# Weight sums, form sums and column statistics moved between engines in the first stage of a 1-core streaming-encoder block

## The chip, the cores and the metric

The kernel runs on one core of a Trainium2 chip (trn2). The metric is the device time of one execution in microseconds; the time before is the median of three runs. The core has five engines that run their own instruction queues in order: TensorE (PE in the profile; PEld are its weight loads), VectorE (DVE), ScalarE (ACT), GpSimd (POOL) and SyncE (SP), the last of which only issues transfers. GpSimd issues transfers too, among them those that add into their destination.

## The reference, cut to what matters

One encoder block on 1024 tokens of width 1024: RMS norm, one wide input projection, windowed attention with sinks on one branch, a chunked gated MLP on the other, two merge gates, an output projection, a residual and a last RMS norm. The change touches the head of the kernel only: the norm, the product for `vs`, its Gelu, and the mean and variance of each token over the 1024 columns of Gelu(vs), which the layer norm ahead of the spatial gating needs.

```python
h = rmsnorm(x, norm_g)
q, k, v, za, u, vs, zs, gm = split(h @ w_in)
v = layernorm(gelu(vs), ln_g, ln_b)          # mean and variance over 1024 columns per token
mixed = einsum('gij,bnjgc->bnigc', masked(w_s), v_blocks) + b_s
sgo = (gelu(u) * mixed * silu(zs)) @ w_sg_out
```

## The kernel before, in words

**Arithmetic.** Every fp32 operand is split into two parts: hi (a cast to fp32r on ScalarE, L177) and lo (the rest, a subtraction on VectorE, L178); a product is three matmuls (hi hi, hi lo, lo hi). Most products of the kernel use a scheme with seven block products in place of eight (Strassen's in Winograd's order); sums of blocks are formed first, by VectorE, by GpSimd, or by a transfer that adds into its destination (`add_to`, L226).

**The head.** The tokens are eight tiles of 128 (x0 to x7). Each is loaded (`load_x`, L575) into a `wr` tile (three buffers in rotation, shared with the weights), squared and summed on ScalarE (`scale_of`, L648), scaled on VectorE (L654), transposed on TensorE (L659), and evicted from PSUM by ScalarE and VectorE: hi and lo parts for the products (L665, L666) and fp32 copies f11, f12, f21, f22 for the block sums (L678; they lie in T_t3l, T_t4h, T_t4l, T_t3h). `vs_gemm` (L682 under it) multiplies tiles 0 to 4 with the first half of the columns. The weights of `vs` are eight tiles of 128x1024: W0 to W3 for the first 512 columns, W4 to W7 for the last.

**The forms.** Then an order written out by hand (`tc.manual_schedule` for TensorE, ScalarE and VectorE) makes the rest: `plain` multiplies tiles 0 and 4 with W4 to W7 (ps_sc), and for the pairs of tiles (1,5), (2,6), (3,7) `take` does five products called t1, t2, t3, b22 and t4, each in two halves c = 0, 1, 36 matmuls in all, with an evicting step behind the second half. Each form needs the split of a token sum (T_t1 = f11 - f12, T_t2 = -(f22 + T_t1), T_t3 = f22 - f12, T_b22, T_t4 = the difference `last` of what then stands in f11 and f21) and of two weight sums. The weight sums live in `chain`: two `s` tiles that start as W4 and W5 and are split and then added to by a transfer (`of_chain(c, nxt)`: split, then add W_nxt): W4, then +W6 (first form), +W0 (second form), +W2 (b22). An add has to wait until the split before it has read the tile. `ask` loads a raw weight or a sum of two into a `wr` tile, `of_raw` splits the next of these.

**Statistics.** `bn_stats` on VectorE (L858) makes the column statistics of a half row of xh (the tile of Gelu(vs)); `bn_aggr` (L1028) joins them. `normalize` (L1040 on VectorE, L1036 on ScalarE) needs all of them, and the mixing matmuls (`mix`, L1075) need the normalized xh. The next stage is the product for u (`gemm_pair`, L396), whose hooks run normalization, the bias of the mixing (`bias_of`) and the mixes.

**What sets the order.** Inside `manual_schedule` the three engines keep the program's order; GpSimd and SP, and all engines outside, are ordered by the scheduler. Transfers that make sums of later weights in DRAM (`early`, L339 on GpSimd's queue, shown as sums<-in_w_dram) are issued one at a time by `part_of_early` and held to a place among TensorE's matmuls (`paced`).

## Time and profile before

| what | value |
|---|---|
| time before | 917.69 us, median of 3 runs (916.05 to 919.14) |
| the profiled execution, its own time | 919.23 us |
| its span, first to last instruction | 917.2 us |
| busy: PE, DVE, ACT, POOL | 894.8, 710.7, 542.1, 162.3 us |
| instructions | 13264 |
| granted clock of TensorE, mean | 0.992 |
| chain that ended last | PE 91%, DMA 4%, DVE 2%, ACT 2%, issue 1% |

The chain is followed back from the last instruction to whatever released each step; TensorE makes up 91% of it, so the kernel is bound by TensorE, and other engines count where TensorE waits for them. In the rows of the profile, `wh` and `wl` are the hi and lo part of a weight, `T_t2h` and `T_t2l` those of the second form's token sum, and so on; `a<-b,c` reads "a is made from b and c"; a row of the timeline gives start, duration, engine, line, operation, shape, count (x) and in square brackets the engine's idle time ahead of it and what ended it. L682 is the matmul helper of the head, L396 that of the later stages.

### The profile page before, as it was taken

The page shows a single profiled execution, that of the slowest core. Times are in us where ns is not written, and L with a number is a line of the kernel's source. Part 1 is how long each engine was busy: PE and PEld are TensorE (multiplying, and loading weights), DVE is VectorE, ACT ScalarE, POOL GpSimd, SP SyncE. Part 2 cuts the span into 40 slices and gives each one's busy share as a digit, 9 for nine tenths or more (in the row PEclk, how much of TensorE's full clock was granted, in tenths as well). Part 3 has the DMA queues.
Part 4 walks back from the last instruction along what each step waited for, and adds up shares of the span by engine and source line. Part 5 has one row for each costly group of instructions (what it writes and reads, how often), then busy time and mean ns, then how long its engine had stood idle before and what let it go on. Part 6 is the DMA issues. An engine that isn't in the chain of part 4 may idle for free.

```text
span 917.2 us, 13264 instructions
## 1 busy us (share of the span) xinstructions
PE 894.8 (98%) x4269; PEld 745.2 (81%) x4269; DVE 710.7 (77%) x1251; ACT 542.1 (59%) x1078; POOL 162.3 (18%) x235
## 2 busy tenths in 40 slices
PE   8986999999999999999999999999999999999997
PEld 6775888888888888888888888888888888878886
DVE  6788895666668687888888888666698699579986
ACT  7765453333444557887878877434476485357444
POOL 2242222223011001222211110011100111210012
PEclk9997999999999999999999999999999999999999
DMA  7895799885878879999999995875568666999623
GB/s 253 233 254 130 207 173 186 176 197 176 272 240 267 275 255 317 261 263 277 239 350 267 260 260 150 299 252 189 167 205 306 222 204 177 243 304 324 207 106 124
DMA packets 131476, 212.39 MB, mean 232 GB/s; under 512 B 12908, under 2 KB 61040, under 8 KB 131408
## 3 DMA queue, kind: packets, MB, share of 16 engines
q1 hardware_dynamic: 108584, 148.36, 50.5%
q0 software_dynamic: 22528, 62.93, 29.3%
q8 instruction: 34, 0.56, 0.2%
q14 instruction: 34, 0.28, 0.1%
q10 hardware_dynamic: 296, 0.27, 0.1%
HBM read 154.76 MB, written 90.31 MB: 267 GB/s over the span
## 4 chain that ended last, share of the span: by engine, by line
PE 91%; DMA 4%; DVE 2%; ACT 2%; issue 1%; POOL 0%; SPq 0%; DVEq 0%; POOLq 0%; ACTq 0%
PE ps_mm L396 43%; PE ps_o L396 26%; PE ps_tp L396 4%; PE ps_sc L1423 3%; DMA wr<-in_w_dram 3%; PE ps_sc L396 2%; PE ps_o L682 2%; PE ps_mm L682 2%; PE ps_tp L1075 2%; PE ps_tp L1504 2%; PE ps_o L1564 2%; DMA s<-in_w_dram 1%; PE ps_o L1572 1%; PE ps_tp L1514 1%; PE ps_sc L682 1%
## 5 line engine op out<-in xcount | busy, mean ns | idle before, releaser
L177 ACT CAST wh<-s 128x1024 fp32r<-128x1024 f32 (+1 forms) x86 | 86.5, 1007 | 88.1 <-PE ps_mm L396 30.2
L178 DVE TENSOR_TENSOR wl<-s,wh 128x1024 fp32r<-128x1024 f32 (+1 forms) x86 | 100.5, 1169 | 19.6 <-ACT wh L177 19.3
L178 DVE TENSOR_TENSOR wl<-wr,wh 128x512 fp32r<-128x512 f32 (+1 forms) x65 | 61.6, 949 | 58.4 <-ACT wh L177 58.3
L177 ACT CAST wh<-wr 128x512 fp32r<-128x512 f32 (+1 forms) x65 | 53.9, 831 | 70.2 <-PE ps_mm L396 36.1
L1464 ACT ACTIVATE pr<-ps_sc,sm 128x192 f32<-128x192 f32 (+2 forms) x128 | 51.3, 408 | 24.3 <-DVE sm L1455 21.6
L339 POOL DMA_DIRECT2D sums<-in_w_dram x48 | 36.8, 846 | 137.7 <-issue 56.4
L396 PE MATMUL ps_o<-T_b22h,wh 128*128 128x512 f32 x148 | 59.0, 398 | 0.0
L396 PE MATMUL ps_o<-T_t1h,wh 128*128 128x512 f32 x148 | 58.0, 392 | 0.0
L396 PE MATMUL ps_o<-T_b22h,wl 128*128 128x512 f32 x148 | 57.8, 391 | 0.0
L396 PE MATMUL ps_o<-T_t1h,wl 128*128 128x512 f32 x148 | 57.8, 390 | 0.0
L396 PE MATMUL ps_o<-T_b22l,wh 128*128 128x512 f32 x148 | 57.8, 390 | 0.0
L396 PE MATMUL ps_o<-T_t1l,wh 128*128 128x512 f32 x148 | 57.7, 390 | 0.0
L396 PE MATMUL ps_mm<-T_t4h,wh 128*128 128x512 f32 (+1 forms) x144 | 55.9, 388 | 1.5 <-DVE x L440 1.5
L396 PE MATMUL ps_mm<-T_t4h,wl 128*128 128x512 f32 (+1 forms) x144 | 55.3, 384 | 0.0
L396 PE MATMUL ps_mm<-T_t4l,wh 128*128 128x512 f32 (+1 forms) x144 | 55.3, 384 | 0.0
L396 PE MATMUL ps_mm<-T_t2h,wh 128*128 128x512 f32 x140 | 55.3, 395 | 0.0
L396 PE MATMUL ps_mm<-T_b11h,wh 128*128 128x512 f32 x140 | 55.1, 393 | 0.0
L396 PE MATMUL ps_mm<-T_b11l,wh 128*128 128x512 f32 x140 | 54.8, 391 | 0.0
L396 PE MATMUL ps_mm<-T_t3h,wh 128*128 128x512 f32 x140 | 54.8, 391 | 0.0
L396 PE MATMUL ps_mm<-T_b11h,wl 128*128 128x512 f32 x140 | 54.6, 390 | 0.0
L396 PE MATMUL ps_mm<-T_t3h,wl 128*128 128x512 f32 x140 | 54.6, 390 | 0.0
L396 PE MATMUL ps_mm<-T_t2h,wl 128*128 128x512 f32 x140 | 54.6, 390 | 0.0
(478 smaller groups left out, 2493.3 us busy)
## 6 DMA issues: line engine op xcount, KB each, us to landing
wr<-in_w_dram SPq DMA_DIRECT2D x80, 256.0 KB
sums<-in_w_dram POOLq DMA_DIRECT2D x24, 512.0 KB, 7.2
s<-sums SPq DMA_DIRECT2D x24, 512.0 KB
wr<-in_w_dram SPq DMA_DIRECT2D x17, 512.0 KB
q_hl<-qhl SPq DMA_DIRECT2D x16, 512.0 KB
q<-q_hl SPq DMA_DIRECT2D x64, 128.0 KB
y_dr<-x POOLq DMA_DIRECT2D x28, 256.0 KB, 6.3
sums<-in_w_dram POOLq DMA_DIRECT2D x24, 256.0 KB, 7.4
```

The source lines that it names most:

```text
L177: hi_casts.append(nc.scalar.copy(hi, src))
L178: return nc.vector.tensor_sub(lo, src, hi.bitcast(F32))
L339: return lambda: paced(nc.gpsimd.dma_start(dst, src, accum_op=op))
L396: mm = nc.tensor.matmul(acc, lt, rt, start=fresh and k == 0 and n == 0, stop=k == 3 and n == 2, skip_group_check=True,)
L682: mm = nc.tensor.matmul(acc, lt, rt, start=first and n == 0, stop=last and n == 2, skip_group_check=True)
L1075: nc.tensor.matmul(pm[:, t * P : (t + 1) * P], xh[:, half * 4 + t, g * P : (g + 1) * P], bias[-1][1][:, g % 2, :], start=True, stop=True,)
L1423: nc.tensor.matmul(sc[:, i, lo:hi], q_of[:, c, i * P : (i + 1) * P], kt[:, f, lo:hi], start=f == 0, stop=f == 1,)
L1464: nc.scalar.activation(st.pr[:, i, place_of(c, lo, hi)], st.sc[c][:, i, lo:hi], AF.Exp, bias=st.nmax[:, c, i : i + 1], scale=-1.0, accum_o ...
L1504: nc.tensor.transpose(st.inner[0:wide, at : at + P], st.pr[:, i, place_of(c, 64 if st.t else P, 192)], ident[:])
L1514: nc.tensor.transpose(st.ends[0:wide, i * P : (i + 1) * P], st.pr[:, i, P : P + wide], ident[:])
L1564: nc.tensor.matmul(st.po[:], lt, rt, start=i == 0, stop=False, skip_group_check=True)
L1572: nc.tensor.matmul(st.po[:, cols(c)], ends[:, c, vs], st.b[:, cols(c)], start=False, stop=c == 1, skip_group_check=True)
```

## The change

Five things are edited; all lie in the head, and the arithmetic of the result is the same apart from rounding.

1. **No sums on GpSimd.** f22 - f12 (two instructions of 128x1024) and the four of `last` (128x512 each) go to VectorE. f11 - f12 is made per token tile (`first_form`, 128x512 each), for tiles 4 to 6 as soon as they are evicted, for tile 7 at the start of the written order.
2. **A tile of its own for the second form's first weight sum.** `apart` is loaded with W4 and has W6 and W0 added when tile 4 is done; after its split W2 is added, and b22 takes it from there. The `s` tile of chain 0 ends with W4 + W6. Chain 1 (W5, +W7, +W1, +W3) stays as it was.
3. **Statistics of tiles 0, 4, 5, 6 and 7 on ScalarE.** Their Gelus give row sums (`accum_out`); `means_of` makes the mean and its negative (small VectorE instructions), `variance_of` squares xh with the negative mean as bias and sums (Square on 128x1024, into a scratch `idle_row`). Tiles 1, 2 and 3 keep bn_stats and bn_aggr. The hooks of the next stage hold three aggregations instead of eight ahead of `normalize`.
4. **Late sums' transfers moved.** Two `part_of_early` go from tile 3 of `vs_gemm`, two of four from tile 4, one from `plain`; `take` issues two per half and three tiles in t3, b22 and t4.
5. **W6 is asked for ahead of x7's load**, and the split of the raw W6 stands ahead of the written order.

The diff, with one line around each edit and without the renaming of a helper for the sinks:

```diff
@@ -723,3 +723,3 @@
             pace[0] = vs_step(part, t, k, *vs_w[k], (0, KC - 1) if t == 4 else (k & 4, k | 3))
-            if k in {3: (0, 4), 4: (0, 2, 4, 6)}.get(t, ()):
+            if t == 4 and k in (0, 4):
                 part_of_early(1)
@@ -812,3 +812,3 @@
     chain = []
-    added = [None]
+    apart = htile([P, D], F32, "apart")
 
@@ -821,5 +821,6 @@
     def of_chain(c, nxt=None):
-        weights.append(vs_weights(chain[c][:]))
+        raw = chain[c] if c < 2 else apart
+        weights.append(vs_weights(raw[:]))
         if nxt is not None:
-            added[0] = add_to(chain[c][:], w[W_VS + nxt])
+            add_to(raw[:], w[W_VS + nxt])
 
@@ -852,5 +853,9 @@
                 of_chain(c, 6 + c)
+            ask(6)
         if t == 4:
-            for c in range(2):
-                ask(6 + c)
+            copy_to(apart[:], w[W_VS + 4])
+            add_to(apart[:], w[W_VS + 6])
+            add_to(apart[:], w[W_VS])
+            ask(7)
+            of_raw()
 
@@ -859,5 +864,23 @@
 
-    def gelu_of(t, n=2, half=0):
-        some = xh[:, t : t + n, half_of(half)]
-        nc.scalar.activation(some, some, AF.Gelu)
+    totals, mean_less = stats[:, :, :, 0], stats[:, :, 0, 1]
+    BY_SUMS = (0, 4, 5, 6, 7)
+    last_gelu = [None]
+
+    def gelu_of(t, half, src=None, n=1, scale=1.0):
+
+        dst = xh[:, t : t + n, half_of(half)] if n > 1 else xh[:, t, half_of(half)]
+        total = totals[:, t, half : half + 1] if t in BY_SUMS else None
+        last_gelu[0] = nc.scalar.activation(
+            dst, dst if src is None else src, AF.Gelu, scale=scale, accum_out=total
+        )
+
+    def means_of(t, n):
+        two, mean = totals[:, t : t + n], mv[:, t : t + n, 0]
+        nc.vector.tensor_add(mean, two[:, :, 0], two[:, :, 1])
+        nc.vector.tensor_scalar_mul(mean_less[:, t : t + n], mean, -1.0 / D)
+        nc.vector.tensor_scalar_mul(mean, mean, 1.0 / D)
+
+    def variance_of(t):
+        var = mv[:, t, 1:2]
+        nc.scalar.activation(idle_row, xh[:, t, :], AF.Square, bias=mean_less[:, t : t + 1], accum_out=var)
 
@@ -866,7 +889,5 @@
 
-    def sum_of(op, dst, a, c, engine=nc.vector):
+    def sum_of(op, dst, a, c):
         for cs in pairs:
-            made = engine.tensor_tensor(dst[:, cs, :], a[:, cs, :], c[:, cs, :], op=op)
-            if engine is nc.gpsimd:
-                after(made, added[0])
+            nc.vector.tensor_tensor(dst[:, cs, :], a[:, cs, :], c[:, cs, :], op=op)
 
@@ -885,3 +906,3 @@
             if c == 3:
-                nc.scalar.activation(xh[:, t, HALF:D], others[t], AF.Gelu)
+                gelu_of(t, 1, others[t])
 
@@ -909,4 +930,4 @@
                 done(p, into[p], xh[:, p + 4, 0:HALF], xh[:, p + 4, HALF:D])
-            if s > 1:
-                part_of_early()
+            if s > 1 and p != 2 + c % 2:
+                part_of_early(1)
 
@@ -920,3 +941,3 @@
         nc.vector.tensor_sub(q2, q2, acc)
-        nc.scalar.activation(q2, q2, AF.Gelu)
+        gelu_of(p + 4, 1)
 
@@ -924,18 +945,17 @@
         nc.vector.tensor_add(q1, q1, acc)
-        nc.scalar.activation(q1, q1, AF.Gelu)
+        gelu_of(p + 4, 0)
 
     def negated(p, acc, q1, q2):
-        nc.scalar.activation(xh[:, p, HALF:D], acc, AF.Gelu, scale=-1.0)
-
-    whole = [(t, 0) for t in range(5)] + [(t, 1) for t in (0, 4, 5, 6, 7)] + [(t, 0) for t in (5, 6, 7)]
-
-    def more_statistics(n):
-        for _ in range(n):
-            statistics(*whole.pop(0))
+        gelu_of(p, 1, acc, scale=-1.0)
 
     others = {t: bank("sc")[:] for t in (0, 4)}
+    def first_form(t):
+        part = f11[:, :, tokens(t)]
+        nc.vector.tensor_sub(part, part, f12[:, :, tokens(t)])
+
+    for t in (4, 5, 6):
+        first_form(t)
     with tc.manual_schedule(engines={mybir.EngineType.PE, mybir.EngineType.Activation, mybir.EngineType.DVE}):
         hb.update(new_b(("t1",)))
-        sum_of(ALU.subtract, f11, f11, f12)
-        of_raw()
+        first_form(7)
         form("t1", f11, (0,))
@@ -943,12 +963,10 @@
         of_raw()
-        part_of_early(1)
         form("t1", f11, (1,))
         plain(1)
-        of_chain(0, 0)
-        gelu_of(0)
+        of_chain(0)
+        gelu_of(0, 0)
         plain(2)
         of_chain(1, 1)
-        sum_of(ALU.subtract, f12, f22, f12, nc.gpsimd)
-        gelu_of(2)
-        gelu_of(4, 1)
+        gelu_of(1, 0, n=3)
+        gelu_of(4, 0)
         plain(3)
@@ -959,14 +977,14 @@
         form("t2", f11)
-        last = [xtile() for _ in range(4)]
-        for c in range(4):
-            nc.gpsimd.tensor_tensor(last[c][:], f11[:, c, :], f21[:, c, :], op=ALU.subtract)
-        more_statistics(2)
-        of_chain(0, 2)
+        of_chain(2, 2)
+        sum_of(ALU.subtract, f12, f22, f12)
         take("t1", 0)
         of_chain(1, 3)
+        last = [xtile() for _ in range(4)]
+        for c in range(4):
+            nc.vector.tensor_sub(last[c][:], f11[:, c, :], f21[:, c, :])
         take("t1", 1, negative)
-        more_statistics(2)
-        of_raw()
         hb.update(new_b(("t3",)))
-        form("t3", f12)
+        form("t3", f12, (0,))
+        of_raw()
+        form("t3", f12, (1,))
         take("t2", 0)
@@ -974,4 +992,3 @@
         take("t2", 1, plus)
-        more_statistics(3)
-        of_chain(0)
+        of_chain(2)
         hb.update(new_b(("t4",)))
@@ -981,2 +998,3 @@
         ask(7, raw=htile([P, D], F32, "g_sb"))
+        idle_row = xtile()[:].bitcast(BF16)
         begin_job()
@@ -984,4 +1002,7 @@
         of_chain(1)
+        means_of(0, 1)
+        means_of(4, 1)
         take("t3", 1, less)
         of_raw()
+        variance_of(0)
         take("b22", 0)
@@ -989,5 +1010,8 @@
         make_sums()
-        more_statistics(3)
+        variance_of(4)
         take("b22", 1, both_terms)
         split_next()
+        means_of(5, 3)
+        for t in (1, 2, 3):
+            statistics(t, 0)
         take("t4", 0)
@@ -995,7 +1019,12 @@
         take("t4", 1, negated)
-    more_statistics(3)
+    of_head = last_gelu[0], splits[-1]
+    for t in (5, 6, 7):
+        variance_of(t)
+    for t in (0, 4):
+        nc.vector.tensor_scalar_mul(mv[:, t, 1:2], mv[:, t, 1:2], 1.0 / D)
+    nc.vector.tensor_scalar_mul(mv[:, 5:8, 1], mv[:, 5:8, 1], 1.0 / D)
...
@@ -1025,4 +1054,3 @@
     def statistics_of(t):
-        if t in (1, 2, 3):
-            statistics(t, 1)
+        statistics(t, 1)
         behind_of[1] = nc.vector.bn_aggr(mv[:, t, :], stats[:, t])
@@ -1056,4 +1084,4 @@
         if p == 0:
-            after(hi_casts[-1], casts[-1])
-            after(rest_of, los[-1])
+            after(hi_casts[-1], of_head[0])
+            after(rest_of, of_head[1])
         rs = bank("sc")
@@ -1097,3 +1125,3 @@
 
-    late.extend(lambda t=t: statistics_of(t) for t in range(NT))
+    late.extend(lambda t=t: statistics_of(t) for t in (1, 2, 3))
     late.append(normalize)
```

What that does to the order, at three places.

VectorE at the second form's token sum, before. T_t3l is f11, T_t2l and T_t2h the split, T_t4h and T_t3h f12 and f22, wl the lo part of a weight, bn the statistics:

```order
L869 TENSOR_TENSOR T_t3l_168<-T_t3h_387,T_t3l_168 128x1024 x2
L173 SCALAR_TENSOR_TENSOR T_t2l_692<-T_t3l_168,T_t2h_691 128x1024 x2
L858 BN_STATS bn_127<-xh_126 128x6 x2
L178 TENSOR_TENSOR wl_710<-s_462,wh_709 128x1024
L178 TENSOR_TENSOR wl_733<-s_464,wh_732 128x1024
L858 BN_STATS bn_127<-xh_126 128x6 x2
L178 TENSOR_TENSOR wl_761<-wr_685,wh_760 128x1024
L178 TENSOR_TENSOR T_t3l_765<-T_t4h_386,T_t3h_764 128x1024 x2
L178 TENSOR_TENSOR wl_789<-wr_688,wh_788 128x1024
L858 BN_STATS bn_127<-xh_126 128x6 x3
L1028 BN_AGGR mv_128<-bn_127 128x2 x2
L178 TENSOR_TENSOR wl_817<-s_462,wh_816 128x1024
```

The same place after; x_727 to x_730 are the four of `last`:

```order
L892 TENSOR_TENSOR T_t3l_168<-T_t3h_388,T_t3l_168 128x1024 x2
L173 SCALAR_TENSOR_TENSOR T_t2l_690<-T_t3l_168,T_t2h_689 128x1024 x2
L178 TENSOR_TENSOR wl_698<-apart_181,wh_697 128x1024
L892 TENSOR_TENSOR T_t4h_387<-T_t3h_388,T_t4h_387 128x1024 x2
L178 TENSOR_TENSOR wl_723<-s_465,wh_722 128x1024
L984 TENSOR_TENSOR x_727<-T_t3l_168,T_t4l_169 128x512
L984 TENSOR_TENSOR x_728<-T_t3l_168,T_t4l_169 128x512
L984 TENSOR_TENSOR x_729<-T_t3l_168,T_t4l_169 128x512
L984 TENSOR_TENSOR x_730<-T_t3l_168,T_t4l_169 128x512
L178 TENSOR_TENSOR T_t3l_757<-T_t4h_387,T_t3h_756 128x1024
L178 TENSOR_TENSOR wl_761<-wr_683,wh_760 128x1024
L178 TENSOR_TENSOR T_t3l_757<-T_t4h_387,T_t3h_756 128x1024
```

The bn_stats between the second form's token sum and its weights are gone, the split of `apart` stands directly behind it, and the sums that were GpSimd's stand behind the first and the second weight split.

GpSimd's queue before, from the adds for the third form's weights (wr) to the adds of W2 and W3 (the last two s):

```order
L226 DMA wr_685<-in_w_dram 128x1024
L226 DMA wr_688<-in_w_dram 128x1024
L226 DMA s_462<-in_w_dram 128x1024
L226 DMA s_464<-in_w_dram 128x1024
L869 TENSOR_TENSOR T_t4h_386<-T_t3h_387,T_t4h_386 128x1024 x2
L962 TENSOR_TENSOR x_699<-T_t3l_168,T_t4l_169 128x512
L962 TENSOR_TENSOR x_700<-T_t3l_168,T_t4l_169 128x512
L962 TENSOR_TENSOR x_701<-T_t3l_168,T_t4l_169 128x512
L962 TENSOR_TENSOR x_702<-T_t3l_168,T_t4l_169 128x512
L1021 MEMSET x_1024 128x128
L226 DMA s_462<-in_w_dram 128x1024
L226 DMA s_464<-in_w_dram 128x1024
```

GpSimd's queue after, from the first adds to the weights on; sums_104 to 106 are the sums of later weights:

```order
L226 DMA apart_181<-in_w_dram 128x1024 x2
L226 DMA s_463<-in_w_dram 128x1024
L226 DMA s_465<-in_w_dram 128x1024
L339 DMA sums_104<-in_w_dram 128x2x512
L339 DMA sums_105<-in_w_dram 128x2x512
L226 DMA wr_683<-in_w_dram 128x1024
L226 DMA wr_686<-in_w_dram 128x1024
L226 DMA s_465<-in_w_dram 128x1024
L226 DMA apart_181<-in_w_dram 128x1024
L226 DMA s_465<-in_w_dram 128x1024
L339 DMA sums_106<-in_w_dram 128x2x512
```

The sums are gone from this queue; the adds of W6 and W0 to `apart` come first in it, and W1's add (the second s_465) stands behind the two for the third form as before, without a second add beside it.

ScalarE around the loads of x7 and W6, before. L648 is the square of a token tile (wr_564 is x7), wr_593 is W6, ps_tp_447 and 454 are the transposes of x5, ps_tp_509 and 516 those of x6:

```order
L648 ACTIVATE wl_140,st_91_497<-wr_495 128x1024
L678 COPY T_t4h_386<-ps_tp_447 128x4x128
L148 ACTIVATE st_92_499<-st_91_497,eps_sb 128x1
L665 CAST T_b22h_384<-ps_tp_454 128x4x128
L648 ACTIVATE wl_140,st_104_566<-wr_564 128x1024
L678 COPY T_t3h_387<-ps_tp_454 128x4x128
L148 ACTIVATE st_105_568<-st_104_566,eps_sb 128x1
L177 CAST wh_607<-wr_593 128x1024
L678 COPY T_t4h_386<-ps_tp_509 128x4x128
L665 CAST T_b22h_384<-ps_tp_516 128x4x128
```

The same place after; wr_533 is W6, wr_563 x7, ps_tp_448 and 455 are x5's transposes, ps_tp_508 and 515 x6's:

```order
L648 ACTIVATE wl_140,st_92_496<-wr_494 128x1024
L177 CAST wh_597<-wr_533 128x1024
L678 COPY T_t4h_387<-ps_tp_448 128x4x128
L665 CAST T_b22h_385<-ps_tp_455 128x4x128
L148 ACTIVATE st_93_498<-st_92_496,eps_sb 128x1
L678 COPY T_t3h_388<-ps_tp_455 128x4x128
L648 ACTIVATE wl_140,st_106_565<-wr_563 128x1024
L148 ACTIVATE st_107_567<-st_106_565,eps_sb 128x1
L678 COPY T_t4h_387<-ps_tp_508 128x4x128
L665 CAST T_b22h_385<-ps_tp_515 128x4x128
```

W6's cast went from behind x7's square and root to ahead of it, and ahead of the evictions of x5 and the root of x6. On SP the load of W6 stands ahead of that of x7, each in the buffer that the other would have had.

10 lines of the change are left out of this document (5 added, 5 removed).

## The prediction

> **What bounds the kernel now.** First the busy time by stretch (columns: TensorE, its weight loads, VectorE, ScalarE, GpSimd, each with its instructions in brackets; then granted clock, DMA share, GB/s), because a kernel whose TensorE is busy in 98% of its span can only be helped where TensorE stands still.
>
> ```profile
> 35.00:48.50 13.50, 10.60 (x56) 8.09 (x56) 6.80 (x16) 7.00 (x15) 3.48 (x5) 1.00 0.99 301
> 67.70:87.30 19.60, 10.72 (x38) 8.29 (x38) 18.45 (x16) 8.62 (x11) 7.06 (x8) 0.74 0.56 117
> 87.30:111.70 24.40, 24.40 (x109) 20.19 (x109) 19.12 (x29) 13.29 (x20) 6.33 (x12) 1.00 0.71 215
> ```
>
> The hole is at 67.7 to 87.3: TensorE works 10.7 of 19.6 us there, at a granted clock of 0.74. A small one is at 35 to 48.5 (2.9 us). Where TensorE is full, as from 87.3 on, no saving on another engine shows. Next, whom TensorE waited for in the whole span, and its own rows around the hole:
>
> ```profile
> PE ps_mm L682 <- DVE wl L178: 4.9, 1, 4.9
> PE ps_mm L682 <- ACT wh L177: 4.0, 1, 4.0
> PE ps_tp L659 <- ACT T_t3h L678: 2.6, 2, 1.4
> ```
> ```profile
> 67.45 0.39 PE L682 MATMUL ps_mm<-wh,T_t1l 128*128 128x512 f32 x1
> 71.79 0.79 PE L682 MATMUL ps_mm<-wh,T_t2h 128*128 128x512 f32 x1 [3.96 <-ACT wh L177]
> 77.50 0.79 PE L682 MATMUL ps_mm<-wl,T_t2h 128*128 128x512 f32 x1 [4.92 <-DVE wl L178]
> 78.10 0.63 PE L682 MATMUL ps_mm<-wh,T_t2l 128*128 128x512 f32 x1
> 87.12 0.39 PE L682 MATMUL ps_mm<-wh,T_t3h 128*128 128x512 f32 x1
> 88.64 2.72 PE ps_o L682 x12
> ```
>
> The two big waits stand at the first matmuls of the second form (T_t2). The last row, from the chain, gives TensorE's pace: 12 matmuls in 2.72 us, 0.227 each. From the last matmul of the first form (67.45) to the first of the third (87.12) are 37 steps: 37 x 0.227 = 8.39 us if nothing waited, and 19.67 as measured. **The hole costs 11.28 us**: 8.88 of waits and 2.4 of matmuls at the lower clock behind them (rows of 0.63 us instead of 0.39).
>
> Why it waited: GpSimd, VectorE and ScalarE in the same microseconds.
>
> ```profile
> 61.24 2.04 POOL L226 DMA_DIRECT2D s<-in_w_dram  x2
> 62.35 5.70 POOL L869 TENSOR_TENSOR T_t4h<-T_t3h,T_t4h 128x1024 f32<-128x1024 f32 x2
> 67.06 5.84 POOL L962 TENSOR_TENSOR x<-T_t3l,T_t4l 128x512 f32<-128x512 f32 x4
> ```
> ```profile
> 58.67 1.23 DVE L178 TENSOR_TENSOR wl<-s,wh 128x1024 fp32r<-128x1024 f32 x1 [0.97 <-ACT wh L177]
> 62.17 12.96 DVE L173 SCALAR_TENSOR_TENSOR T_t2l<-T_t3l,T_t2h 128x1024 fp32r<-128x1024 f32 x2
> 75.05 1.27 DVE L858 BATCH_NORM_STATS2 bn<-xh 128x6 f32<-128x512 f32 x2
> 76.25 2.33 DVE L178 TENSOR_TENSOR wl<-s,wh 128x1024 fp32r<-128x1024 f32 x2
> ```
> ```profile
> 61.07 2.20 ACT L172 ACTIVATE T_t2h<-T_t3l 128x1024 fp32r<-128x1024 f32 x2
> 70.69 1.04 ACT L177 CAST wh<-s 128x1024 fp32r<-128x1024 f32 x1 [7.43 <-DMA s<-in_w_dram]
> 73.18 1.05 ACT L177 CAST wh<-s 128x1024 fp32r<-128x1024 f32 x1 [1.44 <-DMA s<-in_w_dram]
> ```
> ```profile
> L173 DVE SCALAR_TENSOR_TENSOR T_t2l<-T_t3l,T_t2h x2: 1211/6519/11827, 62.2 to 73.9; 128x1024 fp32r<-128x1024 f32 x2
> ```
>
> There are two causes, one behind the other. The weight sum W0+W4+W6 was added into a tile that its earlier split had first to leave, so its add was issued at 61.24 and its cast (ScalarE, behind those of T_t2) began only at 70.69, after 7.43 us of waiting for that transfer. And two like VectorE instructions took 11.83 and 1.21 us: the long one lies from 62.17 to 74.0 over the six sums on GpSimd (62.35 to 72.9). So the lo half of the weight was begun at 76.25 and not at 71.7, where its cast had ended. Taking away one cause alone would leave most of the hole.
>
> **The change, part by part.**
>
> *Sums on VectorE.* The six sums leave GpSimd. Prices and the number for the statistics (VectorE, then ScalarE):
>
> ```profile
> L869 DVE TENSOR_TENSOR T_t3l<-T_t3h,T_t3l 128x1024 f32<-128x1024 f32 x2 | 2.4, 1219 | 0.0
> L178 DVE TENSOR_TENSOR T_t4l<-x,T_t4h 128x512 fp32r<-128x512 f32 x4 | 2.5, 684 | 0.0
> L858 DVE BATCH_NORM_STATS2 bn<-xh 128x6 f32<-128x512 f32 x13 | 8.2, 678 | 0.0
> L648 ACT ACTIVATE wl<-wr x7: 1056/1073/1109, 11.1 to 40.0; 128x1024 f32<-128x1024 f32 x7
> L648 ACT ACTIVATION_READ_ACCUMULATOR wl<-wr x7: 186/202/240, 12.1 to 40.9; 128x1 f32 x7
> ```
>
> VectorE gains 2 x 1.22 + 4 x 0.68 = 5.2 us of sums and loses 11.83 - 1.21 = 10.6 us of standing. The sums stand behind the weight split that the second form waits for (the order in the change's section), so only later splits feel them.
>
> *A place of its own for the weight sum.* The tile "apart" is loaded behind the first two s tiles and added to twice, by my estimate before 40 us; its split waits for no DMA at 64. Its cast comes behind the casts of T_t2 on ScalarE, which end at 63.3 before and about 1 us later now (four gelus with a read of the accumulator at 0.2 each in place of bigger ones without): cast 64.3 to 65.3. VectorE: T_t2 done at 65.5, split of "apart" done at 66.7. TensorE asks at 67.68, 1 us later. The first wait costs nothing then; that ScalarE and VectorE work is under the first form's matmuls.
>
> *What is late next.* The second half of the second form needs chain 1 with W1 added, at 67.68 + 18 x 0.227 = 71.8. Its add waits for the split of the old content (58.67 + 1.23 = 59.9 in the trace), and can be issued at about 60. Adds of this tile take
>
> ```profile
> DMA to landing us min/median/max: 5.3/7.8/11.3
> ```
>
> so it lands between 65.3 and 71.3, 67.8 at the median; the longest was the second of the two issued together at 61.24, and now one of these stands elsewhere. With cast and split (1.05 + 1.22) that is 67.6 to 73.6: from nothing to 1.8 us of wait. The third form's first split then stands behind 2.4 us of T_t4 sums and 2.7 of x sums: 66.7 + 2.4 + 1.2 + 2.7 + 1.2 + 1.2 = 75.4 against 75.8 needed. I book **0.3 us** for both, near the median.
>
> *Statistics.* Ten of sixteen bn_stats go (6 us of VectorE), twelve tiny ones come. ScalarE gets five squares of 128x1024 and ten accumulator reads: 5 x 1.28 + 10 x 0.2 = 8.4 us. A square with a bias per partition is not in the trace; the plain one is 1.07, the nearest with a bias and a scale is the first row here:
>
> ```profile
> 117.98 1.25 ACT L1036 ACTIVATE xh<-xh,st,st 128x1024 f32<-128x1024 f32 x1
> L928 ACT ACTIVATE xh<-ps_o 128x512 f32<-128x512 f32 x2 | 1.2, 592 | 0.0
> ```
>
> so 1.07 to 1.25, and I take 1.07. ScalarE has 11 us free in 87.3 to 111.7. Three squares lie between the last gelus, directly ahead of the copy of x11 that the next stage's third product waits for. When the fourth form has ended, ScalarE still has two of those squares, a gelu, a cast of 1.05 and that copy (0.59 each for gelu and copy, second row): 2.6 + 0.6 + 1.05 + 0.6 = 4.8 us, and TensorE two products of 2.72 us, 5.4. I book nothing; uncovered it costs up to 2 us (rival C).
>
> *Transfers.* SP loads "apart" behind the two s loads, one load and one add more in all (2 x 512 KB). Five copies of the sums of later weights leave the crowded stretch before 52 us and go behind 77, where TensorE is full and their first readers, the pairs made ahead, are a stage and more away. And **W6 is asked for before token tile 7 (x7)**:
>
> ```profile
> 22.13 10.69 SPq L575 DMA_DIRECT2D wr<-in_x_dram  x3
> 36.57 6.14 SPq L229 DMA_DIRECT2D wr<-in_w_dram  x2
> ```
> ```profile
> 39.98 1.06 ACT L648 ACTIVATE wl<-wr 128x1024 f32<-128x1024 f32 x1 [2.85 <-DMA wr<-in_x_dram]
> 44.69 1.05 ACT L177 CAST wh<-wr 128x1024 fp32r<-128x1024 f32 x1 [2.89 <-DMA wr<-in_w_dram]
> ```
>
> Before, x7 was issued at 32.5 and used at 40.0 (7.4 us), W6 at 36.6 and used at 44.7 (8.1). Swapped, W6 is there at about 40 and x7 at 44.0 to 44.7. Now the cast of W6 stands on ScalarE ahead of the evictions of tile 5 and the root of tile 6, so tile 6's scaling goes to about 44; behind it on VectorE the lo part of W6 waits for x7's square too, since it takes the buffer of the squares' scratch. From x7's landing: square and read 1.3, W6's lo 1.2, tile 6's sum and lo 1.4, small steps 0.4, then scaling 1.4 and transposes 0.5 (estimates from the rows of like size above). The transposes now stand inside the plain products, five matmuls in, so six of these (1.4) are done by then: the products run as if begun 4.8 us after x7's landing, at 49.2 for the middle, against
>
> ```profile
> 48.52 0.48 PE L682 MATMUL ps_sc<-wh,T_b11h 128*128 128x512 f32 x1
> ```
>
> The 2.9 us hole of before is in that 48.52 already. If x7 lands at 43 this place gains 0.7, at 47 it loses 3.3. I book a loss of **0.7 us**.
>
> **Sum.** 11.28 gained, 0.3 and 0.7 lost: 10.3 us. The profiled execution took 919.23, so 908.9; the median shown is 1.54 lower, so 907.4.
>
> **A rule of the Trainium skill against the change.** GpSimd's last adds were issued while VectorE was busy without a break:
>
> ```profile
> 77.75 0.86 POOL L226 DMA_DIRECT2D s<-in_w_dram  x1 [4.71 <-DVE wl L178]
> ```
>
> The Trainium skill (SBUF — State Buffer, "SBUF: two separate sides") says that a DMA from the GpSimd queue can lack its descriptors as long as VectorE runs an instruction that holds the port pair they share. By that rule the add of W1 would stand until VectorE pauses (rival D), and the sum would be about 922; that row, 0.86 us beside VectorE's 76.25 to 78.6, speaks against it.
>
> **Rivals.**
> A. *The second wait takes the first one's place*: W1's add lands at 73.1 as before. For it: 512 KB adds share one queue, and the two adds for the third form are ahead of it. Split at 73.1 + 1.05 + 1.22 = 75.4, needed at 71.8 + 0.7 = 72.5: 2.9 us, of which 0.3 is booked; 910.0. Chance 0.13.
> B. *The head*: x7 lands 3 us later than I think, for the DMA share there is 0.99. 910.4. Against: two of the copies of sums between 35 and 46 are gone. Chance 0.15.
> C. *ScalarE holds the mixing*: the first mix on TensorE moves from behind the sixth product of the next stage to behind the fourth, and waits for normalization, which waits for the last squares.
>
> ```profile
> 111.77 2.72 PE ps_mm L396 x12
> 117.80 2.25 DVE L1040 TENSOR_SCALAR xh<-xh,mv,st 128x1024 f32<-128x1024 f32 x3
> 128.33 1.78 PE ps_tp L1075 x16
> ```
>
> Before, tiles 0 to 2 were normalized 8.3 us after that stage began; the new slot of the mix is at 4 x 2.72 + 0.3 = 11.2. 3.8 us of squares put 12.1 there: 0.9 us, with bias and evictions up to 2; 909.4. Chance 0.10.
> D. *Slower*: VectorE's run without a break from 60 on holds W1's add in GpSimd's queue. VectorE stops by itself at the split that needs it, at 66.7 + 2.4 = 69.1; from there 5.3 to 11.3 us of DMA and 2.3 of cast and split: 76.7 to 82.7 against 71.8, and 2.4 us at a lower clock: 7.3 to 13.3. Where the adds of the third form's weights are held ahead of it, half a landing more each (3.9): up to 21. It makes the kernel slower where TensorE loses over 10.6 us there; for the middle, 11.3 and one add ahead, 13.3 + 3.9 gives 907.1 + 17.2 = 924.3, with none ahead 920.4, and I take 922. Against it: the row of 77.75. Chance 0.04.
> E. *The change doesn't do what it says*: VectorE's 11.83 us came from something else than GpSimd's sums. Then 5.2 us of sums stand behind it, 1.2 of bn_stats not ahead; TensorE resumes at 76.3 to 77.5 as before; with the 0.7 of the head and up to 1.2 gained, about 917.5. Against it: the like instruction of 1.21 us, begun when GpSimd had ended. Chance 0.03.
>
> **How the numbers follow.** Forecast 907.4 with 0.55, its own range 905.0 to 909.5 (head from a gain of 0.5 to a loss of 2, W1 from 0 to 1.8). A, B and C lie between 909 and 911; beyond them half of B's tail, D and E stay out. Low end: 917.69 - 11.28 - 1.9 (two thirds of the hole at 35 to 48.5) = 904.5. Range 904.5 to 911.5. Within 0.3% (2.75 us, about what a measurement of this kernel tells from no change) lies E; slower is D: faster 0.93, same 0.03, slower 0.04.
>
> **What would show it.** Right: both T_t2l splits at 1.2 us, a cast of "apart" with no DMA wait, the first matmuls of the second form following those of the first at 0.23 us, granted clock 1.00 there. Each later step is seen in the same rows: W1's landing by the wait of the second cast from s, the head by the start of the plain products (48.5 to 49.7), rival C by a wait ahead of the first mix. Wrong it would be if T_t2l is long again, or if x7's square waits beyond 46.

## The result, and the profile after

The changed kernel takes **908.3 us** (median of four runs, 906.78 to 910.01) against 917.27 us of the kernel before on the same chip: ratio 0.990, 95% interval 0.987 to 0.993. In a second series it took 909.65 against 918.28, ratio 0.991 (0.989 to 0.993). The gain is 9 us (8.6 in the second series). The forecast was 907.4 us, 904.5 to 911.5. The profiled execution took 906.95 us, with a span of 905.2 us; before it was 917.2.

First the stretches around the hole, and the head's small one (columns as before). The hole of 67.7 to 87.3 had TensorE at 10.72 of 19.60 us and the clock at 0.74:

```profile
35.00:48.50 13.50, 9.95 (x50) 7.84 (x50) 9.09 (x22) 7.74 (x16) 1.49 (x2) 1.00 0.99 266
60.00:68.00 8.00, 8.00 (x37) 6.64 (x36) 7.40 (x8) 5.74 (x11) 1.70 (x2) 1.00 0.67 115
68.00:77.00 9.00, 9.00 (x42) 7.44 (x41) 8.90 (x10) 7.10 (x11) 0.85 (x1) 1.00 0.80 149
```

TensorE has no idle time from 60 to 77 and the full clock; the head (35 to 48.5) is worse by 0.65 us. TensorE's waits of the whole span say the same: the two of 4.9 and 4.0 us at L682 are gone, and the three largest in the head are now

```profile
PE ps_tp L659 <- DVE wr L654: 2.2, 1, 2.2
PE ps_tp L659 <- ACT xh L727: 1.6, 1, 1.6
PE ps_tp L659 <- issue: 0.9, 1, 0.9
```

TensorE's first matmuls of the first, second and third form and of the next stage:

```profile
60.13 0.39 PE L682 MATMUL ps_tp<-wh,T_t1h 128*128 128x512 f32 x1
68.30 0.39 PE L682 MATMUL ps_mm<-wh,T_t2h 128*128 128x512 f32 x1
76.45 0.39 PE L682 MATMUL ps_mm<-wh,T_t3h 128*128 128x512 f32 x1
100.94 0.39 PE L396 MATMUL ps_mm<-T_b11h,wh 128*128 128x512 f32 x1
```

From the first form to the next stage are 40.81 us, which is 180 matmuls at 0.2267: nothing is lost. Before, the same rows read 59.52 and 111.60, so 52.08, and **the difference to 40.81, 11.27, is the hole**. This pair of numbers, the start of the first form (the head) and the excess over 40.81 (the forms), is used for every run below.

The start of the first form holds a part that no edit touches. ScalarE's square of tile 1 (x1), ahead of every edit, begins at 11.1 us before, at 10.2 in the changed kernel and, in a second profile of the same changed kernel (control, below), at 11.2. Counted from that square the head takes 48.4 us before and 49.9 after, in both profiles: it loses 1.5 us, and the 0.6 between 59.52 and 60.13 is too small by the earlier start. The head's lengths below are counted from there. The two rows, the changed kernel first:

```profile
L648 ACT ACTIVATE wl<-wr x7: 1059/1073/1121, 10.2 to 44.4; 128x1024 f32<-128x1024 f32 x7
```
```profile
L648 ACT ACTIVATE wl<-wr x7: 1058/1072/1113, 11.2 to 45.4; 128x1024 f32<-128x1024 f32 x7
```

Now VectorE, ScalarE and GpSimd at that place:

```profile
63.05 2.36 DVE L173 SCALAR_TENSOR_TENSOR T_t2l<-T_t3l,T_t2h 128x1024 fp32r<-128x1024 f32 x2 [0.60 <-ACT T_t2h L172]
65.33 1.22 DVE L178 TENSOR_TENSOR wl<-apart,wh 128x1024 fp32r<-128x1024 f32 x1
68.74 1.22 DVE L178 TENSOR_TENSOR wl<-s,wh 128x1024 fp32r<-128x1024 f32 x1
```
```profile
63.87 1.04 ACT L177 CAST wh<-apart 128x1024 fp32r<-128x1024 f32 x1
67.17 1.05 ACT L177 CAST wh<-s 128x1024 fp32r<-128x1024 f32 x1 [2.26 <-PE ps_tp L682]
```
```profile
60.48 0.85 POOL L226 DMA_DIRECT2D s<-in_w_dram  x1 [2.71 <-DVE wl L178]
```

Both splits of T_t2 take 1.2 us (they took 13 together), the cast of `apart` has no wait in brackets, and W1's add, issued at 60.48, has landed when ScalarE is free for its cast at 67.17 (what that cast waited for is a product). The head:

```profile
31.79 1.06 ACT L648 ACTIVATE wl<-wr 128x1024 f32<-128x1024 f32 x1 [2.36 <-DMA wr<-in_x_dram]
38.31 1.05 ACT L177 CAST wh<-wr 128x1024 fp32r<-128x1024 f32 x1 [1.04 <-DMA wr<-in_w_dram]
44.41 1.06 ACT L648 ACTIVATE wl<-wr 128x1024 f32<-128x1024 f32 x1 [2.61 <-DMA wr<-in_x_dram]
```

These are the square of x5, the cast of W6 and the square of x7, each with a wait for its transfer; x5's wait is new.

### The profile page after: what moved, and what is told of

Its sections match the earlier page's. It is cut to its first block, busy times and chain, and to the rows that moved or that the text cites. A ratio compares the mean times of both kernels' runs of the same rounds, so it can differ in the third digit from the quotient of the medians.

```text
span 905.2 us, 13294 instructions
## 1 busy us (share of the span) xinstructions
PE 890.8 (98%) x4269; PEld 742.3 (82%) x4269; DVE 700.1 (77%) x1256; ACT 547.9 (61%) x1098; POOL 152.8 (17%) x230
## 4 chain that ended last, share of the span: by engine, by line
PE 94%; DMA 2%; ACT 2%; DVE 1%; issue 0%; SPq 0%; ACTq 0%
PE ps_mm L396 45%; PE ps_o L396 27%; PE ps_tp L396 4%; PE ps_sc L1451 3%; PE ps_sc L396 2%; DMA wr<-in_x_dram 2%; PE ps_o L682 2%; PE ps_tp L1103 2%; PE ps_tp L1532 2%; PE ps_o L1592 2%; PE ps_mm L682 2%; PE ps_tp L682 1%; PE ps_sc L682 1%; PE ps_o L1600 1%; PE ps_tp L1542 1%; ACT wl L648 1%
## 5 line engine op out<-in xcount | busy, mean ns | idle before, releaser
L177 ACT CAST wh<-s 128x1024 fp32r<-128x1024 f32 (+1 forms) x84 | 84.4, 1006 | 78.2 <-PE ps_mm L396 27.6
L178 DVE TENSOR_TENSOR wl<-s,wh 128x1024 fp32r<-128x1024 f32 (+1 forms) x84 | 98.5, 1173 | 18.6 <-ACT wh L177 18.2
```

Of the source, the lines that this page charges most:

```text
L177: hi_casts.append(nc.scalar.copy(hi, src))
L178: return nc.vector.tensor_sub(lo, src, hi.bitcast(F32))
```

## The experiments

Twelve kernels were run. In the table the intervals are those of the ratio to the kernel before; "first form", "head" (from the square of x1 to the first form) and "excess" are read from each run's one profile as above. The runs were measured in three series, each beside the kernel before, so small differences between series are better read from the ratios.

| run | median us | ratio (95%) | first form at | head us | excess us |
|---|---|---|---|---|---|
| before | 917.7 to 918.4 | 1 | 59.52 | 48.4 | 11.27 |
| control (the change) | 909.65 | 0.991 (0.989-0.993) | 61.15 | 49.9 | 0.0 |
| sums_on_gpsimd | 917.76 | 0.999 (0.998-1.001) | 63.51 | 52.4 | 9.6 |
| no_own_place | 906.07 | 0.988 (0.985-0.991) | 58.00 | 47.0 | 1.2 |
| before_sums_on_vector | 914.31 | 0.995 (0.994-0.997) | 58.69 | 47.6 | 6.0 |
| late_sums_back | 914.07 | 0.995 (0.993-0.997) | 63.91 | 52.8 | 1.8 |
| two_edits | 912.50 | 0.994 (0.993-0.995) | 55.82 | 44.9 | 8.1 |
| stats_on_vector | 909.52 | 0.991 (0.990-0.993) | 63.12 | 53.3 | 0.1 |
| w6_after_x7 | 908.51 | 0.990 (0.988-0.991) | 61.99 | 51.0 | 0.0 |
| w6_split_later | 909.29 | 0.990 (0.988-0.991) | 63.31 | 52.7 | 0.0 |
| add_first | 906.30 | 0.987 (0.985-0.989) | 58.19 | 47.0 | 0.3 |
| add_first_split_later | 905.29 | 0.986 (0.984-0.988) | 56.96 | 47.0 | 1.7 |
| cast_behind_x7 | 903.10 | 0.984 (0.983-0.985) | 54.69 | 45.0 | 1.3 |

One profile is a coarse measure of the head: stats_on_vector and sums_on_gpsimd, whose edits all lie behind the head, show 53.3 and 52.4 us where the changed kernel shows 49.9. A difference of 3 us between two single heads is therefore shown only where the medians, or a second pair of runs, say the same.

**control**, the changed kernel unchanged.

> The changed kernel again, unchanged, to have its gain within a narrower interval and to see whether its times lie in two groups (two of its four were 906.8 to 907.0, two 909.6 to 910.0). Theory (the hole of 67.7 to 87.3 is gone, nothing of it came back elsewhere): 907 to 908.5, ratio 0.988 to 0.991, TensorE with no wait over 0.5 us between 60 and 101. Rival (an execution can lose 3 us at a place that the profiled one doesn't show): times again in two groups 3 us apart.

TensorE has no wait over 0.5 us between 60 and 101, as the theory says. The median of 909.65 lies above its 907 to 908.5, and the ratio at its upper end. The rival is not out: of the ten times of the changed kernel in both series three lie at 906.78 to 907.62 and seven at 909.07 to 910.59, and both profiles were taken in executions of the three. No trace of the seven was kept. The nearest is stats_on_vector's (909.78), which loses its 3 us in the head; the kernel before spreads over as much (914.84 to 920.62 in 22 runs).

**sums_on_gpsimd**, the six sums on GpSimd again.

```diff
+        sum_of(ALU.subtract, f12, f22, f12, nc.gpsimd)
...
-        sum_of(ALU.subtract, f12, f22, f12)
-            nc.vector.tensor_sub(last[c][:], f11[:, c, :], f21[:, c, :])
+            nc.gpsimd.tensor_tensor(last[c][:], f11[:, c, :], f21[:, c, :], op=ALU.subtract)
```

> The changed kernel with one part undone: the six sums (two of 128x1024, four of 128x512) on GpSimd again, behind W1's add; the place of its own for the weight sum stays. Theory (GpSimd's sums stretched VectorE's split of the second form from 1.21 to 11.83 us, and each cause alone keeps most of the hole): the long instruction is back, 8 to 11 us; apart's split, behind it on VectorE, starts at 73 to 75 and not at 65.3, TensorE waits from 67.5 to about 76 and runs at a lower clock for some us behind: 914 to 918. Rival 1 (the long instruction came from something else than GpSimd): no wait, 907 to 909, with 2.4 + 2.7 us less on VectorE. Rival 2 (the DMA wait for the weight sum was the whole hole, the long instruction lay under it): 908 to 911.

The whole gain is lost, 8.1 us by the medians. One group of VectorE in this run, and GpSimd in the same microseconds (in the group, minimum, median and maximum in ns):

```profile
L894 DVE TENSOR_TENSOR T_t3l<-T_t3h,T_t3l x2: 1217/4823/8429, 63.7 to 64.9; 128x1024 f32<-128x1024 f32 x2
```
```profile
64.67 5.06 POOL L894 TENSOR_TENSOR T_t4h<-T_t3h,T_t4h 128x1024 f32<-128x1024 f32 x2
69.51 2.69 POOL L985 TENSOR_TENSOR x<-T_t3l,T_t4l 128x512 f32<-128x512 f32 x2
73.37 4.39 POOL L985 TENSOR_TENSOR x<-T_t3l,T_t4l 128x512 f32<-128x512 f32 x2 [1.17 <-DVE T_t3l L894]
```
```profile
75.37 0.80 PE L682 MATMUL ps_mm<-wh,T_t2h 128*128 128x512 f32 x1 [3.54 <-ACT wh L177]
78.90 0.80 PE L682 MATMUL ps_mm<-wl,T_t2h 128*128 128x512 f32 x1 [2.73 <-DVE wl L178]
```

This time the long instruction is not the split of T_t2 but the sum ahead of it (8.43 us, its twin 1.22): the VectorE instruction that starts within 0.2 us of GpSimd's first sum (64.86 and 64.67 here, 62.17 and 62.35 before) stands until GpSimd pauses at 72.2. Both waits at the second form are back. Rivals 1 and 2 are out.

**no_own_place**, the second form's first weight sum in chain 0's tile again.

```diff
-    apart = htile([P, D], F32, "apart")
-        raw = chain[c] if c < 2 else apart
+        raw = chain[c % 2]
-            copy_to(apart[:], w[W_VS + 4])
-            add_to(apart[:], w[W_VS + 6])
-            add_to(apart[:], w[W_VS])
-        of_chain(0)
+        of_chain(0, 0)
```

> The changed kernel with another part undone: the second form's first weight sum is again added into chain 0's tile after its split, apart is gone; the sums stay on VectorE. Theory (the second cause by itself): W0's add is issued at about 58 to 60 behind the first form's split and lands 5.6 to 11.5 us later, its cast then begins at 66 to 71 and not at 63.9; the second form's first matmul, due at 67.2, is ready at 68.3 to 73.3: 1 to 6 us of wait, 909 to 914 less what the head wins without apart's three transfers (up to 2 us, since x5's load, 10.5 us now, is no longer beside them). Rival (with VectorE free the add is early enough): 906 to 908. Rival (each cause alone keeps most of the hole, as the prediction has it): 914 to 918.

Not slower but 3.6 us faster than control (the intervals just overlap; add_first, below, without the place either, ends just below control's). GpSimd, ScalarE and TensorE in the forms, and in the head the stretch and x7's square:

```profile
56.94 1.18 POOL L226 DMA_DIRECT2D s<-in_w_dram  x1
```
```profile
64.98 1.05 ACT L177 CAST wh<-s 128x1024 fp32r<-128x1024 f32 x1 [3.15 <-DMA s<-in_w_dram]
```
```profile
67.34 0.50 PE L682 MATMUL ps_mm<-wl,T_t2h 128*128 128x512 f32 x1 [0.76 <-DVE wl L178]
```
```profile
35.00:48.50 13.50, 11.46 (x63) 9.15 (x62) 9.04 (x20) 7.77 (x15) 1.49 (x2) 1.00 0.60 193
```
```profile
41.37 1.06 ACT L648 ACTIVATE wl<-wr 128x1024 f32<-128x1024 f32 x1
```

W0's add is issued at 56.94 and not at 61.24 as before, and costs 1.2 us of excess where the place of its own costs none. But the head takes 47.0 us and not 49.9 (the same 47.0 in add_first and add_first_split_later, without the place too): the DMA share in 35 to 48.5 is 0.60 and not 0.99, and x7's square has no wait and comes 3 us earlier. The mechanism that was expected is there (a wait of 0.76 us, below the 1 to 6 expected); what the three transfers of the place cost the head was larger. By the time alone the run is the first rival's, 906 to 908.

**before_sums_on_vector**, the kernel before with the six sums on VectorE (the same edit, in the old kernel).

> The kernel before with one part done: the six sums go from GpSimd to VectorE, at the places that they have in the changed kernel; the rest is as before. Theory (two causes one behind the other): VectorE's split of the second form takes 1.2 us twice; what is left is the DMA wait for W0's add, issued at 61.2 beside W1's: cast at 70 to 71, its lo part at 71 to 73, and 2 to 4 bn_stats of 0.68 us in VectorE's way, so 4 to 6 us of wait and 1 us of lower clock: 911 to 914. Rival (each cause alone keeps most of the hole): 915 to 918. Rival (the six sums are dearer on VectorE than the standing they end): above 918.

```profile
61.07 2.05 POOL L226 DMA_DIRECT2D s<-in_w_dram  x2
```
```profile
68.96 1.04 ACT L177 CAST wh<-s 128x1024 fp32r<-128x1024 f32 x1 [6.51 <-DMA s<-in_w_dram]
```
```profile
70.06 0.50 PE L682 MATMUL ps_mm<-wh,T_t2h 128*128 128x512 f32 x1 [3.05 <-ACT wh L177]
```

4 us faster, at the upper end of the theory; the excess falls from 11.3 to 6.0. Of what is left, 3.05 us is the wait shown, for W0's add, issued at 61.07 together with W1's; 0.8 is a second wait, and the rest, about 2 us, goes with the lower clock behind them (0.86 from 70 to 82). So one cause alone takes away half of the hole, not little of it.

**late_sums_back**, the changed kernel with the five copies of late sums where they were.

```diff
-            if t == 4 and k in (0, 4):
+            if k in {3: (0, 4), 4: (0, 2, 4, 6)}.get(t, ()):
-            if s > 1 and p != 2 + c % 2:
-                part_of_early(1)
+            if s > 1:
+                part_of_early()
         of_raw()
+        part_of_early(1)
```

> The changed kernel with the five copies of late sums back between 31 and 52 us, where the kernel before has them. Theory (they share the DMA engines with x7 and with the adds): x7 lands 1 to 3 us later, the first form starts at 61 to 63, W1's add is late by 0 to 2: 1 to 4 us slower, 910.5 to 913. Rival (as the prediction booked: nothing): within 0.5 us of the unchanged one, 909 to 910. Also to be seen: whether the wait of 1.5 us at 790 to 815, which the kernel before has and the changed one hasn't, comes back with them.

4.4 us slower than control by medians, 4.0 by the ratios, and no time of the six overlaps control's. ScalarE at x7's square and at the cast of the chain with W1, and two of TensorE's waits:

```profile
46.76 1.06 ACT L648 ACTIVATE wl<-wr 128x1024 f32<-128x1024 f32 x1 [4.61 <-DMA wr<-in_x_dram]
...
74.87 1.05 ACT L177 CAST wh<-s 128x1024 fp32r<-128x1024 f32 x1 [6.20 <-DMA s<-in_w_dram]
```
```profile
PE ps_tp L659 <- ACT xh L727: 3.6, 1, 3.6
...
PE ps_mm L396 <- DVE x L440: 0.8, 1, 0.8
```

x7 lands 1.3 to 2.4 us later than in the two profiles of the changed kernel, W1's add, issued at 65.5 and not 60.5, lands at 74.8; the head is 2.9 us longer (52.8 and 49.9) and the forms lose 1.8. This is the theory's side, beyond its upper end of 913. The second wait stands at 790 to 815. The kernel before has 1.5 us there and before_sums_on_vector 1.1, both with the copies in the early places; with the copies moved it is 0.3 us in add_first and absent elsewhere. How the early copies bring it about was not followed.

**two_edits**, the kernel before with the sums on VectorE and the late sums moved.

> The kernel before with two parts done: the six sums on VectorE (914.31 us by itself) and the five copies of late sums moved behind 77 us; no place of its own, bn_stats and the order of W6 and x7 as before. Theory (what late_sums_back lost, 914.07 against 909.65, is the same here): 908.5 to 910.5, W0's add landed by 66, first form at 57 to 58.5. Rival (these two edits are the whole change, and statistics and W6's order bring nothing): 906 to 907, as without a place of its own. Rival (the late sums cost so much only beside the transfers of a place of its own): 913 to 914.

1.8 us below before_sums_on_vector, less than expected, and above every range but the last rival's, which it misses by half a microsecond. The head is the shortest of all, level with that of cast_behind_x7 (45.0), and 2.7 us shorter than in before_sums_on_vector (44.9 and 47.6): what the moved copies are worth in the head, seen from the other side. But the excess is 8.1 and not 6.0: 2.3 at the second form's first matmul, 2.8 behind it (a wait of 0.8 and the lower clock), and 3.0 of a new wait at the next stage. ScalarE there, the chain, and TensorE's wait:

```profile
101.81 0.40 ACT L177 CAST wTh<-wT 128x256 fp32r<-128x256 f32 x1 [10.99 <-POOL wT L1047]
```
```profile
92.10 9.36 DMA wT<-in_sg_w_dram
```
```profile
PE ps_mm L396 <- ACT wh L177: 2.8, 1, 2.8
```

ScalarE stands 11 us at the cast of the mixing weights, whose transfer takes 9.36 us (a short fill of zeros on GpSimd behind it is what the row names), with the last three Gelus and the next stage's weight behind it. The changed kernel orders this cast behind the last Gelu of the head (`of_head`), and the wait isn't there. That this order is what removes it was read, not tried alone.

**stats_on_vector**, the statistics of all tiles by bn_stats again (`BY_SUMS = ()`, the former calls in their former places).

> The changed kernel with the third edit undone: all sixteen half rows by bn_stats on VectorE at the places of before, no squares and no row sums on ScalarE, eight aggregations ahead of normalization. Theory (two bn_stats, 1.27 us, stand again ahead of the split of apart, which had 0.8 us to spare): 0.5 to 1 us of wait at the second form, up to 1 at the first mix; 910 to 911.5. Rival (nothing on the path): 909 to 910. Rival (the squares had cost something on ScalarE): 907.5 to 909.

The same as control, against the theory: by themselves the statistics on ScalarE bring nothing and cost nothing that can be told. The split of `apart`, two bn_stats later, begins at 69.14 and is done at 70.4, TensorE asks at 71.28 (this run's head was later); so it still had 0.9 us to spare.

**w6_after_x7**, the fifth edit undone.

```diff
-            ask(6)
         if t == 4:
...
+            ask(6)
             ask(7)
-            of_raw()
...
         first_form(7)
+        of_raw()
```

> The changed kernel with the fifth edit undone: W6 asked for behind x7's load and split in the written order, its cast behind x7's square on ScalarE. Theory of the prediction (the edit loses 0.7 us): first form at 59 to 59.8 in place of 60.3, no wait for tile 6's transposes; 908 to 909 against 909.65 of the unchanged one. Rival (x7's load then falls together with the adds to the place of its own, 31 to 45 us, and lands no earlier): 909 to 911. Rival (the adds of the third form's weights and of W1 behind it come later): a wait ahead of the second form's second half, 911 to 913.

Between the theory and no difference: 1.1 us below control, with overlapping intervals. By the profile neither holds, since TensorE's wait in the head didn't go, it changed its cause:

```profile
41.59 1.06 ACT L648 ACTIVATE wl<-wr 128x1024 f32<-128x1024 f32 x1 [4.80 <-DMA wr<-in_x_dram]
```
```profile
44.73 1.09 PE L659 MATMUL ps_tp<-ident,wr 128*128 128x128 f32 x4 [4.45 <-DVE st L153]
```

x7, asked for at 32.4, lands only at 41.6 (44.4 in the changed kernel). Behind its square on ScalarE stands an eviction of tile 5, and behind that on VectorE the second half of tile 6's scaling, for which TensorE waits. So the first form starts at 61.99 and not at 59 to 59.8, and the gain of 1.1 us is not the one that the theory gave a reason for.

**w6_split_later** and **add_first_split_later**, with only `of_raw()` moved to where w6_after_x7 has it, on the changed kernel and on add_first.

> The changed kernel with one half of the fifth edit undone: W6 is still asked for ahead of x7, but split in the written order, behind x7's steps. Theory of the prediction (W6's cast holds tile 6's root and its lo part x7's): tile 6's transposes come 2 to 4 us earlier than 43.3, x7 still lands at 44 to 44.5 and its transposes at 48 and not 49.4; the first form starts at 59 to 59.5 (60.3 in the changed kernel): 0.8 to 1.3 us faster, 907 to 908 where the unchanged one had 909.65. Rival (x7's landing rules, since its load waits for a buffer until 38.3): no change. Rival (the adds behind it in GpSimd's queue come late): slower by 1 to 3.

> The run add_first with, in addition, the split of the raw W6 in the written order again, behind x7's steps (its load stays ahead of x7's). Theory (W6's cast, which waits for its DMA on ScalarE ahead of tile 6's root, costs the 2.0 us wait of TensorE at 42.97 in the version without a place of its own): that wait goes, the first form starts 1 to 2 us earlier, 903 to 904.5. Rival (W6's buffer then comes free later, so the adds of the third form and of W1 are later too): a wait ahead of the second or the third form, 906 or more.

Neither can be told from its base (909.29 and 909.65; 905.29 and 906.30). Neither put its theory to the test: the scheduler left W6's cast on ScalarE ahead of tile 6's root (the square root in its norm, L148), and only the lo part on VectorE moved.

**add_first**, no_own_place with W0's add ordered ahead of the second add for the third form's weights.

```diff
+            made = add_to(raw[:], w[W_VS + second])
+            if second == 5:
+                after(made, first_add[2])
```

> The version without a place of its own (906.07 us), with one order changed on GpSimd: W0's add into chain 0's tile goes ahead of the second add for the third form's weights (it stood behind it, issued at 56.94, while the split that it needs was done at 55.34). Theory (what is left of the second cause is only the add's place in GpSimd's queue): W0's add issued at 55.4 to 56, landed at 63 to 64 and not 64.9, its split done before TensorE asks at 66.2, so the 0.76 us wait at 67.34 is gone: 904.5 to 905.5, about 1 us below the version without it. Rival (the landing is set by the DMA engines' load, not by the issue): unchanged, 906.

The wait of 0.76 us at 67.34 is gone, the excess goes from 1.2 to 0.3; the time can't be told from no_own_place (906.07). In its head the rest is plain:

```profile
38.15 1.05 ACT L177 CAST wh<-wr 128x1024 fp32r<-128x1024 f32 x1 [2.01 <-DMA wr<-in_w_dram]
40.06 0.30 ACT L148 ACTIVATE st<-st,eps_sb 128x1 f32<-128x1 f32 x1
```
```profile
43.13 0.63 PE L659 MATMUL ps_tp<-ident,wr 128*128 128x128 f32 x4 [1.87 <-ACT st L148]
```

W6's cast waits for its transfer with tile 6's root behind it, and TensorE waits for that root.

**cast_behind_x7**, add_first with that cast held behind x7's square.

```diff
             of_raw()
+            after(hi_casts[-1], squares[7])
```

> The run add_first (no place of its own, W0's add first; 906.30 us) with W6's cast held behind x7's square on ScalarE; in add_first_split_later the cast had stayed where it was and only the lo part had moved, so that its expectation was not put to the test. Theory (that cast, waiting 2 us for its DMA ahead of tile 6's root, makes TensorE's wait of 1.9 us at 43.13): the root of tile 6 at 37 and not 40, the wait gone, the first form at 56.3 to 57 in place of 58.35; 904 to 905 if the adds keep up. Rival (x7's landing takes over at once): 905.5 to 906.5. Rival (chain 0's add is then late by as much as the forms are early): a wait ahead of the second form, 906.

903.10 us, ratio 0.984 (0.983 to 0.985): the fastest of all, 1.6% below the kernel before and some 6 us below the changed one. Root and cast in this run:

```profile
34.63 0.29 ACT L148 ACTIVATE st<-st,eps_sb 128x1 f32<-128x1 f32 x1
...
40.62 1.04 ACT L177 CAST wh<-wr 128x1024 fp32r<-128x1024 f32 x1
```

The root comes at 34.6 and not 40.1, TensorE has no wait in the head, and the first form starts at 54.69, 3.5 us earlier than in add_first. Of these, 1.5 us were there before the edit could act, as the first squares show (add_first, then this run):

```profile
L648 ACT ACTIVATE wl<-wr x7: 1059/1073/1109, 11.2 to 41.5; 128x1024 f32<-128x1024 f32 x7
```
```profile
L648 ACT ACTIVATE wl<-wr x7: 1059/1075/1107, 9.7 to 38.9; 128x1024 f32<-128x1024 f32 x7
```

The head itself is 2.0 us shorter (47.0 and 45.0), which is the wait of 1.87 us and what I had put on it. The medians differ by 3.2, the ratios by 2.8 us, and the profiles don't say where the rest comes from. 1.3 us of excess, small waits ahead of the third form and the next stage, are left.

## Why the prediction was right, and where its steps were not

1. *The hole costs 11.28 us and goes.* Right: 11.27 by the landmarks, and 0.0 left.
2. *Two causes, one behind the other.* Right on both mechanisms. GpSimd's sums are shown in both directions: put back, 9.6 us of excess return (8.1 us by the medians); taken out of the kernel before, 5.3 go (4.0). "Taking away one cause alone would leave most of the hole" holds where GpSimd's sums stay (9.6 of 11.3 is left with all other edits made); where they alone go, 6.0 is left, about half.
3. *The split of `apart` done at 66.7, 1 us ahead of TensorE.* Right: 66.5 and 68.3. But the step took for granted that the place of its own was what made the weight sum early. It was not needed: with the other four edits W0's add costs 1.2 us in the old tile, and 0.3 with its place in GpSimd's queue mended.
4. *W1's add and the third form's split, 0.3 us.* 0.0 measured; rival A didn't occur in the changed kernel. It did in late_sums_back (cast at 74.87 after 6.2 us of waiting).
5. *Statistics, nothing.* Right (909.52 and 909.65); rival C is out, TensorE has no wait at the first mix.
6. *The head, a loss of 0.7 us, through x7 behind W6.* The number looks right in the profile (60.13 and 59.52), but that is luck: counted from the square of x1 the head loses 1.5 us, and 0.9 were won by an earlier start that the change has no part in. x7 landed at 44.4, as booked (44.0 to 44.7). What the step left out are the three transfers of `apart`: without them the head is 2.9 us shorter (no_own_place: x5 and x7 earlier). The other part of the step, W6's cast that holds tile 6's root, was named there as a delay of tile 6's scaling to 44 (42.4 measured); taken away by itself, without `apart`, it is worth 2.0 us of the head.
7. *"Five copies of late sums leave the crowded stretch", nothing booked.* **This step failed.** Put back, they cost 4 us (4.4 by medians, 4.0 by ratios): 2.9 in the head and 1.8 in the forms by the profile. Taken out of the kernel before with the sums on VectorE, they are worth 2.7 us in the head, of which 1.8 is left in the time. I had priced the copies where they went and not where they left: the stretch with a DMA share of 0.99, in which x7 and the chain's adds wait.

So the total is partly luck. In the head a cost of about 3 us for `apart` and a gain of about 3 for the late sums' transfers, both booked at nothing, nearly cancel. Both numbers are read from single profiles; the medians of no_own_place and late_sums_back agree with their signs. The gain of 1.5 us at 790 to 815 wasn't foreseen either; with it the two profiled spans differ by 12.0, where the medians differ by 9. The profiled executions stand near the ends of their spreads (919.23 in 914.84 to 920.62, 906.95 in 906.78 to 910.59). Where the longer executions of the changed kernel lose their 2 to 3 us more no trace of it shows; if it is in the head, as in stats_on_vector, the head's loss there is 4 us or more.

Rival D (the adds held while VectorE runs without a break) didn't occur: W1's add was issued at 60.48 in 0.85 us and was landed at 67.17. That doesn't test the rule behind it, since no run shows whether VectorE's instructions in that stretch are of the kind that holds what the issue needs. Rival B didn't occur either (x7's square waits until 44.4, 45.4 in control). Rival E is out by sums_on_gpsimd.

## What to carry to other kernels

Price a transfer that leaves a crowded stretch like one that enters it: here, at a DMA share of 0.99, five copies of 512 KB that went were worth some 3 us of the head, and a buffer "of its own" that had to be filled there cost as much as they gave. Before a sum gets a tile of its own, look at what stands ahead of its transfer in the queue that issues it; one line of order did here what the tile did, without its transfers. A cast that waits for a transfer on an engine that works in order holds everything behind it: put it behind the small steps that others wait for (2.0 us of the head here). And before two profiles are compared at a landmark, compare them at a row ahead of every edit: here that row alone moved by up to 1.5 us.
